# A two-layer hybrid trunk on one core: decay rows of the last x and z block from another queue, gates before weights, one combined pair less

## The chip, the core and the metric

The kernel runs on one core of one Trainium2 chip. A core has four engines that compute, each with its own list of instructions that it runs in order: TensorE (PE in the profile; its weight loads are PEld), VectorE (DVE), ScalarE (ACT) and GpSimd (POOL). SyncE (SP) only starts loads and stores. Loads can also be started from ScalarE's and GpSimd's lists. The metric is the device time of one execution in microseconds; lower is better. The median of the runs is compared.

## What is computed

The reference is a decoder trunk of two layers over 256 tokens of width 2048, in float32. Only its first layer's mixer is touched. Cut to that:

```python
proj = (xn @ w_in).astype(f32)
q, k, v, o, ig, fg, z, xbc, dt = jnp.split(proj, offs, axis=-1)
# eight mLSTM heads
hm = mlstm_chunkwise(q, k, v, i_pre, f_pre)
hm = rms_norm(hm, mlstm_norm) * jax.nn.sigmoid(o)
# 32 SSD heads
xbc = jax.nn.silu(causal_depthwise_conv(xbc, ssd_conv_w, ssd_conv_b))
y = ssd_chunked(xs, dt, a, bm, cm) + ssd_d[:, None] * xs
y = rms_norm(y * jax.nn.silu(z), ssd_norm)
mixed = jnp.concatenate([hm, y], axis=-1)
return mixed @ w_out
```

Behind it come the residual sum, a SwiGLU network of width 5632, a second layer with block attention (one block here, so plain causal attention), and a second SwiGLU network.

## The kernel before

**Products.** Every matrix product keeps float32 accuracy by splitting each operand into a high and a low part (`split`, L143 to L149: a cast on ScalarE and a subtraction on DVE) and adding three products (L303 to L305). Weights are fetched in pairs of two row groups of 128 by two column strips of 512. `weights` (L251) issues the loads and then the casts (L270) and subtractions (L275) of a pair. `block` runs over the eight pairs of a product and follows a plan, a string with one letter a pair. P is the direct form: 24 products of 512 columns. S is a combined form with seven block products in place of eight (21 products). For an S pair, sums of weights are also needed: SP loads one quarter, POOL loads another onto it with an accumulating load (L260, L261), and DVE makes two more additions (L285, L287). Sums of the activations are needed too (`activation_sums`, L235: four subtractions of 128 columns on DVE, a cast on ScalarE and a subtraction on DVE).

**Banks.** Four banks of PSUM take the direct products of a block, four others the extra products of the S pairs. Small work in between (turns of 128x128 blocks, scores, outputs of heads) uses these latter four when no S pair is at work.

**Order.** The program is written in order, and small jobs are queued with `later(wait, ...)`: they are written out after so many more pairs. While S pairs are at work, these jobs are held. A planner then orders each engine's list when the kernel is built. It takes the work that it believes ready, the earliest in the program first; `tc.high_priority(offset=n)` counts an instruction as written n earlier. The splitting of weights has an offset of 800, the emptying of banks 1600. Tiles come from a fixed number of slots by tag (three for sk, which holds q, k, activation sums and some decay rows; ten for s); who wants a slot waits until its last user is done.

**The first layer's mixer** runs in this order: B and C columns (two blocks), x and z columns (four blocks, `xz_block`), q and k of the first four heads, the output projection of the SSD part, then v, o (gate), q and k, v, o for the mLSTM heads, and the output projection of the mLSTM part (`project(w_out, 0, mx, PLAN["w2"], done1)`: two blocks of 1024 output columns).

**Decay rows.** `decay_rows` (L651) fetches, for two heads, their row of cumulated decays from a scratch tensor in HBM and spreads it over all 128 partitions, in two loads of 256 KB and 128 KB. DVE then adds the causal mask (L659), ScalarE takes the exponential (L664, L665), DVE multiplies by the step sizes and the scores of B and C (L710). For each block s of x and z, `ssd_decay` (L702) is written out four times, from the third pair of the next block on, so eight loads a block. All are issued from POOL's queue. The same block also has `x_pair`, in which TensorE turns the columns of x (L466), ScalarE and DVE convolve (L470, L476, L480, L481), and TensorE turns them back (`p_xs`, L699).

**Gates.** `o_block` (L840) multiplies the o columns into the heads. `gathered` completes the four tiles of 128 tokens by 512 columns, ScalarE takes the tanh (L850), DVE makes (tanh + 1) times the head (L851). `turn_strip` queues for each strip of 512 columns two jobs of `transpose_split` (L215): eight turns on TensorE, then copies with gain (L229), casts and subtractions. They give the pairs 0 to 7 of `mx`, two a strip; the first `o_block` makes 0 to 3, the second 4 to 7. A pair named in `mx.sums` (L774) gets its activation sums at once; another one's are made by `summed` when its S pair is first met (which first adds high and low part again, L205). `project` (L869) asks for the sums of all S pairs of the second block as soon as the first block's products are in.

Of the kernel before, what the change touches and what calls it, by code (L numbers as in the profile page):

```python
# [12 lines left out]
OP = mybir.AluOpType  # L13
# [4 lines left out]
P = 128  # L18
T = 256
NT = T // P  # L20
# [8 lines left out]
MH, MDK, MDV = 8, 128, 256  # L29
# [6 lines left out]
SPACE = {"raw": 6, "sum": 2, "wh": 6, "wl": 6, "xa": 8, "sk": 3, "s": 10, "vh": 2, "ph": 1}  # L36
PLAN = {
    "bc": "PPPPPPPP", "xz": "PPPPPPPP", "qk0": "PPPPPPPP", "w1": ("PSPSPSPP", "PSPSPSPP"),
    "v0": "PPPSPSSP", "o": "PPPSPSSP", "qk1": "PPPSPSSP", "v1": "PPPSPSSP", "w2": ("PPPSPSSP", "PPPSPSSP"),
    "x": "PSPSPSSP", "x0": "PPPSPSSP", "down4": ("PSPSPSSP", "PSPSPSSP"), "down3": ("PSPSPP", "PSPSPP"),  # L40
    "av0": "PPPSPSSP", "aq": "PPPSPSSP", "av1": "PPPSPSSP", "wo": ("PPPPPPPP", "PPPSPSSP"),
}
# [19 lines left out]
def hybrid_trunk(ctx: ExitStack, tc: tile.TileContext, a: dict, out: bass.AP):  # L62
    nc = tc.nc
# [16 lines left out]
    def home(tag):  # L80
        return lambda shape, name, dt=F32: big.tile(shape, dt, tag=tag, name=name, bufs=SPACE[tag])

    xa_home, sk_home, s_home, vh_home = home("xa"), home("sk"), home("s"), home("vh")
    ph_home = home("ph")

    def t2(shape, name, dt=F32):
        return tmp.tile(shape, dt, tag="tmp", name=name, bufs=9)
# [42 lines left out]
    G_MIX0, G_FFN0, G_MIX1, G_FFN1, G_ML, G_SS, G_CB = 0, 16, 32, 48, 64, 80, 96  # L130
# [32 lines left out]
    def later(wait, name, fn, *args):  # L163
        pending.append((clock[0] + wait, len(pending), name, fn, args))
# [13 lines left out]
    def need(name):  # L178
        if any(q[2] == name for q in pending):
            assert not held[0], name  # L180
            run_until(lambda p: not any(q[2] == name for q in pending))
# [64 lines left out]
    def turn_strip(kt, s, src, gcol, wait, step=0):  # L246
        for i in range(2):
            later(wait + i * step, (kt.name, 2 * s + i), transpose_split, kt, 2 * s + i,
                  [x[:, i * T:(i + 1) * T] for x in src], gcol)
# [130 lines left out]
    def gathered(F, pre):  # L380
        for i in (0, 2, 1, 3):
            if pre is None:
                yield i // 2, i % 2, F[i]
            else:
                with tc.high_priority(offset=1600):
                    (nc.vector.tensor_sub if i == 2 else nc.vector.tensor_add)(pre[i], F[i], pre[i])
                yield i // 2, i % 2, pre[i]
# [34 lines left out]
    def first_pair(src, turns_after, warm):  # L422
        raw = []
        for w, col in src:
            raw.append(home("raw")([P, 2, STRIP], "raw"))
            nc.sync.dma_start(raw[-1], w[:2 * P, col:col + STRIP].rearrange("(a p) f -> p a f", p=P))
        b = xt0.pair(0)
        pt = aux_bank("p_tr")
        with tc.issue_after(turns_after):
            for i in range(2):  # L430
                for t in range(NT):
                    turned = nc.tensor.transpose(pt[:, i * T + t * P:i * T + (t + 1) * P],
                                                 xin[t][:, i * P:(i + 1) * P], ident).ins
        with tc.issue_after(turned):
            warm_up(warm)
        pair = pt.rearrange("p (a b) -> p a b", a=2)
        high = [home("wh")([P, 2, STRIP], "wh", F32R) for _ in raw]
        low = [home("wl")([P, 2, STRIP], "wl", F32R) for _ in raw]

        def staged(s, k):  # L440
            with tied(last[0], cast[0]):
                split(high[s][:, k, :], low[s][:, k, :], raw[s][:, k, :])
            cast[0], last[0] = fresh

        for k in range(2):
            g = pv[:, G_MIX0 + k:G_MIX0 + k + 1]
            with tied(last[0], cast[0]) if k else ExitStack():
                split(b[:, k, 0, :], b[:, k, 1, :], pair[:, k, :], g)
            cast[0], last[0] = fresh
            staged(0, k)  # L450
        for k in range(2):
            staged(1, k)
        return [[(h[:, k, :], l[:, k, :]) for k in range(2)] for h, l in zip(high, low)]
# [57 lines left out]
    with tc.high_priority(offset=2000):  # L511
        first = first_pair(((w_in, C_B), (w_in, C_C)), rows_turned, WARM[1])
# [72 lines left out]
    scr = drp.tile([SH + MH, T], F32, name="scr")  # L585
# [62 lines left out]
    later(2, "gates", gate_chain)  # L648
    later(8, "gates", gate_columns)

    def decay_rows(first, home):  # L651
        need("gates")
        rb = home([P, 2, W3], "rows2")
        for lo, l0, n in ((0, 0, T), (T, P, P)):
            nc.gpsimd.dma_start(rb[:, :, lo:lo + n],
                                bass.AP(tensor=scr.tensor, offset=scr.offset + first * T + l0,
                                        ap=[[0, P], [T, 2], [1, n]]))
        for lo in (0, T):
            nc.vector.tensor_add(rb[:, :, lo:lo + P], rb[:, :, lo:lo + P],  # L659
                                 mask_sl[:, None, :].to_broadcast([P, 2, P]))  # L660
        return rb

    def decay(e, bias):
        nc.scalar.activation(e[:, :T], e[:, :T], AF.Exp, bias=bias[0])  # L664
        nc.scalar.activation(e[:, T:], e[:, T:], AF.Exp, bias=bias[1])  # L665
        return e
# [7 lines left out]
    def xz_block(s):  # L674
        got = block(((w_in, C_X + s * STRIP), (w_in, C_Z + s * STRIP)), xt0, 0, PLAN["xz"])
        tok = [None] * NT
        zg = sk_home([P, NT, STRIP], "zg")
        for t, i, src in gathered(*got):
            if i == 0:
                tok[t] = scaled(t, src, r0_)  # L680
            else:
                th = t2([P, STRIP], "thz")
                with tc.high_priority(offset=1600):
                    nc.scalar.activation(th, src, AF.Tanh, scale=rh0[:, t:t + 1])
                    nc.scalar.activation(zg[:, t, :], src, AF.Copy, scale=rh0[:, t:t + 1])
                nc.vector.scalar_tensor_tensor(zg[:, t, :], th, 1.0, zg[:, t, :], op0=OP.add, op1=OP.mult)
        y = vh_home([P, NT, STRIP], "y")
        for j in range(2):
            later(1 + j, ("x", s), x_pair, s, j, [x[:, j * T:(j + 1) * T] for x in tok], y)
        for j in range(4):  # L690
            later(2 + j, ("y", s), ssd_decay, s, j, y, zg)
# [10 lines left out]
    def ssd_decay(s, j, y, zg):  # L702
        need("cb")
        h0 = 8 * s + 2 * j
        es = decay_rows(MH + h0, s_home if j % 2 else sk_home)
        for hh in range(2):
            h = h0 + hh
            e = decay(es[:, hh, :], [ncols[:, t, CCS + h:CCS + h + 1] for t in range(NT)])
            for t, sl in ((0, slice(0, T)), (1, slice(T, W3))):
                nc.vector.scalar_tensor_tensor(e[:, sl], e[:, sl], cols[:, t, CDT + h:CDT + h + 1],  # L710
                                               cb[h // 8][:, (h // 4) % 2, sl], op0=OP.mult, op1=OP.mult)
        later(1, ("y", s), ssd_out, s, j, es, y, zg)
# [58 lines left out]
        nc.scalar.copy(dst, pt.rearrange("p (a b) -> p a b", a=2))  # L771

    mx = KT("mx", KD, s_home, {j: sk_home for j in range(KD // 2)})
    mx.sums = {5: None, 6: None}  # L774
    vh, em = {}, {}

    def qk_block(g, plan):
# [62 lines left out]
    def o_block(g, plan):  # L840
        for i in range(2):
            later(1 + g + i, ("hm", g), mlstm_out, 2 * g + i)
            later(min(2 + g + i, 3), ("hm", g), mlstm_norm, 2 * g + i)
        got = block(((w_in, C_O + 2 * g * STRIP), (w_in, C_O + (2 * g + 1) * STRIP)), xt0, 0, plan)
        need(("hm", g))
        gate = {}
        for t, i, src in gathered(*got):
            th = t2([P, 2, MDV], "tho") if got[1] is None else src.rearrange("p (a b) -> p a b", a=2)
            with tc.high_priority(offset=1600 if got[1] is None else 400):
                nc.scalar.activation(th, src.rearrange("p (a b) -> p a b", a=2), AF.Tanh, scale=rh0[:, t:t + 1])  # L850
            nc.vector.scalar_tensor_tensor(th, th, 1.0, vh[2 * g + i][:, t, :, :MDV], op0=OP.add, op1=OP.mult)  # L851
            gate[i, t] = th.rearrange("p a b -> p (a b)")
        for i in range(2):
            turn_strip(mx, 2 * g + i, [gate[i, t] for t in range(NT)], G_ML, 2)

    xr_ = xin

# [41 lines left out]
    project(w_out, D, sx, PLAN["w1"])  # L899
    v_block(0, PLAN["v0"], 1)  # L900
    o_block(0, PLAN["o"])
    qk_block(1, PLAN["qk1"])
    v_block(1, PLAN["v1"], 3)
    o_block(1, PLAN["o"])
    xt1, ss1, done1 = next_x("1", G_FFN0, {1: vh_home, 3: vh_home, 5: sk_home, 6: ph_home})
    project(w_out, 0, mx, PLAN["w2"], done1)
# [255 lines left out]
```

## Time and profile before

| | |
|---|---|
| median of 3 runs | 2551.51 us |
| lowest and highest | 2548.26 and 2552.74 us |
| the profiled execution | 2548.43 us |
| its span, first to last instruction | 2546.7 us |
| mean granted clock of TensorE | 0.998 |
| moved by DMA | 631.51 MB, mean 248 GB/s |
| loads of decay rows from POOL's queue | 20 of 256 KB and 20 of 128 KB |

Times in the rows are microseconds from the first instruction. A row of the order of time has the start, the duration, the engine, the line, the operation, what it writes and reads, and how many such instructions follow one another; in square brackets stand the idle time of the engine before it and what ended it. An engine's name with a q is its queue: it issues a load and does no computing. A row of waits has the engine and line that waited, what it waited for, the sum, the count and the longest. A row of a window has the window, its length, the busy time and count of PE, PEld, DVE, ACT and POOL, the granted clock, the share of the 16 DMA engines, and GB/s.

### The profile page before, as it was taken

To read this page: it belongs to the slowest core of one execution; us is meant where nothing else is said; L and a number is where in the kernel's file an instruction comes from. 1 tells how busy PE (TensorE), PEld (TensorE's weight loads), DVE (VectorE), ACT (ScalarE), POOL (GpSimd) and SP (SyncE) were. 2 spreads that over 40 slices of the span, in tenths; PEclk is the share of its full clock that TensorE was granted. 3 is DMA by queue.
4 is the path that set the end of the run, shared out by engine and by line. 5 is a ranking of instruction groups with operands and counts; after the bars stand their busy time and mean duration, and the time that the engine had idled before them with its cause. 6 is when DMAs were issued, how large, how long until landed. Compare 5 with 4: busy or idle time off the path is not lost.

```text
span 2546.7 us, 34498 instructions
## 1 busy us (share of the span) xinstructions
PE 2525.5 (99%) x11553; PEld 2083.3 (82%) x11553; DVE 2237.2 (88%) x2978; ACT 1601.3 (63%) x2160; POOL 366.8 (14%) x452
## 2 busy tenths in 40 slices
PE   9999999999999999999999999999999999999998
PEld 8888878888878888888888888888888888888887
DVE  6877778978799999999999888988899999999998
ACT  6566656566667665566656666656676656665664
POOL 2101211111111111111111111110011111111110
PEclk9999999999999999999999999999999999999999
DMA  8656668878778999999999887876689999999995
GB/s 281 185 167 189 195 182 257 259 224 254 224 222 252 277 273 283 278 272 276 273 290 270 262 249 230 243 229 208 191 243 282 265 289 275 277 266 296 291 267 175
DMA packets 333665, 631.51 MB, mean 248 GB/s; under 512 B 27256, under 2 KB 29824, under 8 KB 333488
## 3 DMA queue, kind: packets, MB, share of 16 engines
q1 hardware_dynamic: 278928, 527.71, 62.1%
q0 software_dynamic: 53376, 99.76, 22.3%
q8 instruction: 91, 1.49, 0.2%
q10 hardware_dynamic: 1184, 1.84, 0.2%
q14 instruction: 86, 0.70, 0.1%
HBM read 627.07 MB, written 2.14 MB: 247 GB/s over the span
## 4 chain that ended last, share of the span: by engine, by line
PE 95%; DVE 3%; DMA 1%; issue 1%; ACT 0%; POOL 0%; SPq 0%; POOLq 0%; DVEq 0%; ACTq 0%
PE acc_f L303 24%; PE acc_f L305 24%; PE acc_f L304 24%; PE acc_e L303 6%; PE acc_e L305 6%; PE acc_e L304 6%; PE p_tr L215 2%; DVE wl L275 1%; PE p_y L725 1%; PE p_qt L770 0%; PE p_num L814 0%; DMA raw<-in_l_ffn_down 0%; ACT wh L270 0%; DMA rows<-scr 0%; PE p_o L1038 0%
## 5 line engine op out<-in xcount | busy, mean ns | idle before, releaser
L270 ACT CAST wh<-raw 128x1024 fp32r<-128x1024 f32 (+1 forms) x1084 | 1049.5, 982 | 644.4 <-PE acc_f L305 283.8
L275 DVE TENSOR_TENSOR wl<-raw,wh 128x1024 fp32r<-128x1024 f32 (+1 forms) x1084 | 1211.3, 1135 | 189.2 <-ACT wh L270 177.4
L303 PE MATMUL acc_f<-wh,x 128*128 128x512 f32 x1168 | 457.0, 391 | 0.0
L305 PE MATMUL acc_f<-wh,x 128*128 128x512 f32 x1168 | 456.8, 391 | 0.0
L304 PE MATMUL acc_f<-wl,x 128*128 128x512 f32 x1168 | 456.8, 391 | 0.0
L270 ACT CAST wh<-sums 128x1024 fp32r<-128x1024 f32 x174 | 183.0, 1052 | 149.8 <-PE acc_f L305 87.4
L303 PE MATMUL acc_f<-wh,xa 128*128 128x512 f32 x678 | 270.1, 399 | 0.8 <-ACT wh L145 0.8
L305 PE MATMUL acc_f<-wh,xa 128*128 128x512 f32 x678 | 265.1, 391 | 0.0
L304 PE MATMUL acc_f<-wl,xa 128*128 128x512 f32 x678 | 264.8, 391 | 0.0
L305 PEld LDWEIGHTS acc_f<-wh,x 128*128 128x128 f32 x1168 | 219.4, 188 | 44.9
L304 PEld LDWEIGHTS acc_f<-wl,x 128*128 128x128 f32 x1168 | 219.5, 188 | 44.7
L303 PEld LDWEIGHTS acc_f<-wh,x 128*128 128x128 f32 x1168 | 219.4, 188 | 44.5
L275 DVE TENSOR_TENSOR wl<-sums,wh 128x1024 fp32r<-128x1024 f32 x174 | 212.1, 1219 | 27.3 <-ACT wh L270 26.9
L303 PE MATMUL acc_e<-wh,sk 128*128 128x512 f32 x522 | 206.3, 395 | 0.1
L304 PE MATMUL acc_e<-wl,sk 128*128 128x512 f32 x522 | 203.6, 390 | 0.0
L305 PE MATMUL acc_e<-wh,sk 128*128 128x512 f32 x522 | 202.7, 390 | 0.0
L261 POOL DMA_DIRECT2D sums<-in_l_ffn_gate x86 | 74.4, 865 | 765.7 <-DMA sums<-in_l_ffn_up 413.7
L305 PEld LDWEIGHTS acc_f<-wh,xa 128*128 128x128 f32 x678 | 127.5, 188 | 27.2
L304 PEld LDWEIGHTS acc_f<-wl,xa 128*128 128x128 f32 x678 | 127.8, 189 | 25.7 <-DVE wl L146 0.4
L303 PEld LDWEIGHTS acc_f<-wh,xa 128*128 128x128 f32 x678 | 127.6, 188 | 25.9 <-ACT wh L145 1.0
L285 DVE TENSOR_TENSOR raw<-raw,sums 128x512 f32<-128x512 f32 x174 | 118.9, 683 | 8.4 <-DMA sums<-in_l_ffn_down 5.8
L303 PEld LDWEIGHTS acc_e<-wh,sk 128*128 128x128 f32 x522 | 98.0, 188 | 29.4 <-ACT xg L226 6.8
(336 smaller groups left out, 4075.6 us busy)
## 6 DMA issues: line engine op xcount, KB each, us to landing
raw<-in_l_w_in SPq DMA_DIRECT2D x177, 512.0 KB, 4.7
raw<-in_l_ffn_gate SPq DMA_DIRECT2D x176, 512.0 KB, 6.2
raw<-in_l_ffn_down SPq DMA_DIRECT2D x136, 512.0 KB, 7.1
raw<-in_l_ffn_up SPq DMA_DIRECT2D x90, 512.0 KB, 6.5
sums<-in_l_ffn_up SPq DMA_DIRECT2D x172, 256.0 KB, 4.5
raw<-in_l_w_qkv SPq DMA_DIRECT2D x78, 512.0 KB, 6.4
raw<-in_l_w_out SPq DMA_DIRECT2D x52, 512.0 KB, 5.9
sums<-in_l_ffn_gate POOLq DMA_DIRECT2D x86, 256.0 KB, 6.8
```

The lines of the kernel that those rows point to most:

```text
L215: turned = nc.tensor.transpose(pt[:, i * T + t * P:i * T + (t + 1) * P], src[t][:, i * P:(i + 1) * P], ident)
L261: nc.gpsimd.dma_start(sums[:, i, :], other, accum_op=OP.add)
L270: cast[0] = nc.scalar.copy(h[:, :n, :], of[:, :n, :]).ins
L275: last[0] = nc.vector.tensor_sub(l[:, :n, :], of[:, :n, :], h[:, :n, :].bitcast(F32)).ins
L285: nc.vector.tensor_add(b[:, 1, :], b[:, 0, :], sums[:, 0, :])
L303: nc.tensor.matmul(dst, ah, bh, start=start, stop=False, **kw)
L304: nc.tensor.matmul(dst, ah, bl, start=False, stop=False, **kw)
L305: nth[0] = nc.tensor.matmul(dst, al, bh, start=False, stop=stop, **kw).ins
L725: nc.tensor.matmul(py[:, o0:o0 + SHD], e[:, lo:lo + P], y[:, st, hs], start=st == 0, stop=st == t, skip_group_check=True)
```

## The change

The two loads of `decay_rows` take the queue as a parameter: POOL's as before, but ScalarE's for the last x and z block (s == 3). In `o_block` the tanh and the product get one priority, 1200, where the tanh had 400 (1600 in a plan without S, which isn't used for it) and the product none; both now stand ahead of the splitting of weights. For the first gate block the second strip is turned one pair later than the first. In the first block of the mLSTM part's output projection pair 6 is direct, so that two pairs are combined, 3 and 5; the second block keeps three. The pairs whose activation sums are made at once are 3 and 5, not 5 and 6.

```diff
-    "v0": "PPPSPSSP", "o": "PPPSPSSP", "qk1": "PPPSPSSP", "v1": "PPPSPSSP", "w2": ("PPPSPSSP", "PPPSPSSP"),
+    "v0": "PPPSPSSP", "o": "PPPSPSSP", "qk1": "PPPSPSSP", "v1": "PPPSPSSP", "w2": ("PPPSPSPP", "PPPSPSSP"),
...
-    def decay_rows(first, home):
+    def decay_rows(first, home, queue=nc.gpsimd):
...
-            nc.gpsimd.dma_start(rb[:, :, lo:lo + n],
+            queue.dma_start(rb[:, :, lo:lo + n],
...
-        es = decay_rows(MH + h0, s_home if j % 2 else sk_home)
+        es = decay_rows(MH + h0, s_home if j % 2 else sk_home, nc.scalar if s == 3 else nc.gpsimd)
...
-    mx.sums = {5: None, 6: None}
+    mx.sums = {3: None, 5: None}
...
-            with tc.high_priority(offset=1600 if got[1] is None else 400):
+            with tc.high_priority(offset=1200):
                 nc.scalar.activation(th, src.rearrange("p (a b) -> p a b", a=2), AF.Tanh, scale=rh0[:, t:t + 1])
-            nc.vector.scalar_tensor_tensor(th, th, 1.0, vh[2 * g + i][:, t, :, :MDV], op0=OP.add, op1=OP.mult)
+                nc.vector.scalar_tensor_tensor(th, th, 1.0, vh[2 * g + i][:, t, :, :MDV], op0=OP.add, op1=OP.mult)
...
-            turn_strip(mx, 2 * g + i, [gate[i, t] for t in range(NT)], G_ML, 2)
+            turn_strip(mx, 2 * g + i, [gate[i, t] for t in range(NT)], G_ML, 2 + i * (1 - g))
```

More of the change, by code (lines that the diff above doesn't have):

```diff
@@ L654, in decay_rows @@
         for lo, l0, n in ((0, 0, T), (T, P, P)):
-            nc.gpsimd.dma_start(rb[:, :, lo:lo + n],
-                                bass.AP(tensor=scr.tensor, offset=scr.offset + first * T + l0,
-                                        ap=[[0, P], [T, 2], [1, n]]))
+            queue.dma_start(rb[:, :, lo:lo + n],
+                            bass.AP(tensor=scr.tensor, offset=scr.offset + first * T + l0,
+                                    ap=[[0, P], [T, 2], [1, n]]))
         for lo in (0, T):
```

## The prediction

> **What bounds the kernel now.** I read the page first, then the list of waits on TensorE (PE), then the order of time on each engine at the places that list names.
>
> ```profile
> span 2546.7 us, 34498 instructions
> PE 95%; DVE 3%; DMA 1%; issue 1%; ACT 0%; POOL 0%; SPq 0%; POOLq 0%; DVEq 0%; ACTq 0%
> ...
> PE p_xs L699 <- DVE xs L481: 5.6, 1, 5.6
> PE p_tr L215 <- DVE pre L851: 2.7, 7, 0.8
> PE acc_f L303 <- ACT wh L270: 1.9, 2, 1.1
> ```
>
> The chain that ends last is 95% TensorE: the kernel is a row of matrix products, and a change pays only where TensorE stands, or in the number of its products. It stands at few places, and the three longest entries of the waits are one for each part of this change: the turning of the convolved x (p_xs), the turning of the gated heads (p_tr from pre), and the first output block (acc_f waiting for a cast). Busy time hides some of the loss, since the ends of products are modelled, so I measure every stop from the starts.
>
> ```profile
> 307.59 0.39 PE L303 MATMUL acc_f<-wh,xa 128*128 128x512 f32 x1
> ...
> 312.12 0.39 PE L305 MATMUL acc_f<-wh,xa 128*128 128x512 f32 x1
> ...
> 277.23 0.60 PE L699 MATMUL p_xs<-ident,xs 128*128 128x128 f32 x4
> ...
> 327.20 0.39 PE L305 MATMUL acc_f<-wh,xa 128*128 128x512 f32 x1
> 333.23 1.09 PE L699 MATMUL p_xs<-ident,xs 128*128 128x128 f32 x4 [5.63 <-DVE xs L481]
> ...
> 336.16 0.40 PE L305 MATMUL acc_f<-wh,xa 128*128 128x512 f32 x1
> ...
> 334.00:336.00 2.00, 2.00 (x7) 1.61 (x6) 2.00 (x5) 0.63 (x2) 0.00 (x0) 0.50 1.04 214
> ```
>
> The first two rows are the first and last of 21 products in a row: 20 steps in 4.53 us, so one product of 512 columns costs 0.2265 us. The third row is the turn p_xs one x/z block earlier, with no wait before it. In the last block TensorE is free for it at 327.20 + 0.23 = 327.43 and starts at 333.23: **5.80 us** lost. Then the granted clock is 0.50 (last row): from 333.23 to 336.16 four turns and five products take 2.93 us, where four turns at 0.109 (below) and five products make 1.57: another **1.36 us**. Together 7.16 us.
>
> **Part 1: the decay rows.** Why is DVE late there, and only there?
>
> ```profile
> 255.82 5.77 POOL L655 DMA_DIRECT2D rows<-scr  x8
> ...
> 306.96 0.70 POOL L141 TENSOR_TENSOR rrg<-rs,mhalf 128x2 f32<-128x2 f32 x1 [13.40 <-DVE rs L140]
> 312.25 1.83 POOL L261 DMA_DIRECT2D sums<-in_l_w_out  x2 [4.58 <-DMA sums<-in_l_w_out]
> 313.98 4.42 POOL L655 DMA_DIRECT2D rows<-scr  x6
> 319.48 0.71 POOL L655 DMA_DIRECT2D rows<-scr  x1 [1.08 <-DMA sums<-in_l_w_out]
> ...
> 322.20 0.43 DVE L659 TENSOR_TENSOR rows<-rows,phase 128x256 f32<-128x256 f32 x1 [5.65 <-DMA rows<-scr]
> ...
> 332.40 0.68 DVE L481 SCALAR_TENSOR_TENSOR xs<-thc,cv 128x512 f32<-128x512 f32 x1
> ```
>
> In the block before, all eight row loads leave POOL's queue in one stretch at 255.82. One block is 51.8 us long (the p_xs above comes at 277.23, so its like is due at about 329), and the same point here is 307.6, just as POOL ends its power at 307.66. But here POOL's next entry is the accumulating load of the first combined pair of the following projection, which waits for SP's plain load to land; the rows leave 6.3 us late, at 313.98, the last two later still. DVE has the mask addition of the rows (L659) at the head of its list and stands 5.65 us, and all that follows on DVE, up to xs at 332.40 + 0.68, runs without a break. So each microsecond that the first rows land earlier is one microsecond less on TensorE, until 5.80 are gone.
>
> The change takes these eight issues off POOL (5.77 us of its time, which nobody waits for) and puts eight on ScalarE. What they cost there, and when they land:
>
> ```profile
> DMA to landing us min/median/max: 4.6/6.8/9.4
> ...
> 2328.11 1.04 ACT L270 CAST wh<-raw 128x1024 fp32r<-128x1024 f32 x1
> 2328.69 0.33 ACTq L1061 DMA_DIRECT2D gf<-in_final_norm  x1
> 2329.05 0.61 ACT L270 CAST wh<-raw 128x512 fp32r<-128x512 f32 x1
> ...
> 255.00:268.00 13.00, 13.00 (x63) 10.75 (x62) 8.97 (x17) 11.57 (x20) 6.42 (x9) 1.00 0.87 258
> ...
> 313.00:327.00 14.00, 14.00 (x67) 11.50 (x66) 7.47 (x13) 7.96 (x14) 6.82 (x10) 1.00 0.89 263
> ```
>
> The first row is of the rows' own loads. A load issued from ScalarE's queue (2328.69) runs under the cast before it, and the next cast follows without a gap: 8 x 0.33 = 2.6 us of issue, nothing of it on the path as long as casts or copies lie beside it, 2.6 us of ScalarE if that cover is gone. The unknown is where in ScalarE's list the planner puts them. At best they go where POOL was free, 307.7, and land at 312.3 to 317.1: the stop vanishes. At worst they go behind the copies that empty the banks at the end of the block, 314 or later, and land no earlier than now: nothing gained. DVE needs them at 322.20 - 5.80 = 316.4. Nothing in the trace says which, so I take the middle, 310.8, and the median landing, 6.8: 317.6, so 1.2 us stays, too short a stop for the slow clock, of which I see nothing behind stops of about 1 us. Gain 7.2 - 1.2 = **6.0**, ends 0 and 7.2, and a loss in the last rival below. The waiting instructions behind such a load on ScalarE would be these same bank copies and the casts, and TensorE waits for both.
>
> On the landing, the Trainium skill speaks against the change: "DMA: Bandwidth & Descriptors", section "Issuing engines are not separate DMA queues", says that loads from ScalarE, SP and GpSimd run on the same 16 DMA engines and interleave, and that another issuer saves only the time of issuing. The share of 0.89 in the last row above fits it. By that rule alone the gain would be the issue delay, 6.3 us at most, and nothing if the bytes are the limit: the first rival.
>
> **Part 2: gates ahead of weights.**
>
> ```profile
> 558.62 0.29 PE L215 MATMUL p_tr<-ident,pre 128*128 128x128 f32 x1
> ...
> 562.14 0.48 PE L303 MATMUL acc_f<-wh,xa 128*128 128x512 f32 x1
> ...
> 696.20 0.39 PE L305 MATMUL acc_f<-wh,mx 128*128 128x512 f32 x1
> ...
> 700.45 0.48 PE L303 MATMUL acc_f<-wh,mx 128*128 128x512 f32 x1
> ...
> 739.78 0.87 PE p_tr L215 x8
> ...
> 551.44 1.94 ACT L850 ACTIVATE pre<-pre,rh 128x512 f32<-128x512 f32 x3
> 557.84 1.29 DVE L851 SCALAR_TENSOR_TENSOR pre<-pre,v 128x512 f32<-128x512 f32 x2
> ```
>
> Eight turns cost 0.87 us undisturbed (0.109 each), sixteen 1.74. After the first gate block they take 562.14 - 558.62 = 3.52: **1.78** lost; after the second, 700.45 - (696.20 + 0.23) = 4.02: **2.28** lost. The tanh is done at 553.4, but the DVE product (L851) comes at 557.84, behind the splitting of weights. With one priority above the weights' 800, both come first and the turns find their input some 3 us ahead. The weights move back by four tanh (1.94 / 3 = 0.65 each) and four products (0.65 each), 2.6 us on each engine; the pair being split there is used one pair later, at least 5 us away (24 x 0.2265), so I cost this at nothing; uncovered, it is 2.6 us per block.
>
> In the first half the second strip is turned one pair later, immediately before the first combined pair: same eight turns, but its copies out of two banks now meet products that want these banks. Undisturbed that is nothing; the bound above is one strip's copies, four of about the size of a tanh, 2.6 us. I take 0.5, near the lower end, since a combined pair begins with three products into a bank that the turns don't use. Gain 1.78 + 2.28 - 0.5 = **3.6**, ends -1.1 and 4.1.
>
> **Part 3: one combined pair less, sums made early.**
>
> ```profile
> 713.26 0.39 PE L305 MATMUL acc_e<-wh,mx 128*128 128x512 f32 x1
> ...
> 714.40 0.50 PE L303 MATMUL acc_f<-wh,mx 128*128 128x512 f32 x1 [0.75 <-ACT wh L270]
> ...
> 716.99 0.50 PE L303 MATMUL acc_f<-wh,mx 128*128 128x512 f32 x1 [1.13 <-ACT wh L270]
> ...
> 703.51 0.68 DVE L205 TENSOR_TENSOR xg<-mx 128x512 f32<-128x512 f32 x1
> ...
> 713.65 0.28 DVE L238 TENSOR_TENSOR sf<-xg 128x128 f32<-128x128 f32 x1
> ...
> 716.85 0.62 ACT L145 CAST sk<-sf 128x512 fp32r<-128x512 f32 x1
> ...
> L275 DVE TENSOR_TENSOR wl<-sums,wh 128x1024 fp32r<-128x1024 f32 x174 | 212.1, 1219 | 27.3 <-ACT wh L270 26.9
> L285 DVE TENSOR_TENSOR raw<-raw,sums 128x512 f32<-128x512 f32 x174 | 118.9, 683 | 8.4 <-DMA sums<-in_l_ffn_down 5.8
> ```
>
> From 713.26 to 716.99 four products are issued in 3.73 us instead of 0.91: **2.8** lost. DVE has three sets of activation sums to make inside this block; that of pair 3 starts at 703.51 and its cast comes at 716.85. Pair 6 taken directly needs 24 products for 21: +3 x 0.2265 = **0.7** on TensorE. DVE drops from 3 x 1.22 + 3 x 0.68 to 2 x 1.22 for that pair (three whole and one half subtraction, the addition at L285 and its like at L287), 3.3 us less. Pair 3's sums go three blocks earlier, pair 6's to the start of the second output block, each 4 x 0.28 + 0.68 = 1.8 us of DVE and 0.62 of ScalarE, where the waits of TensorE name nothing but the turns. Pair 3's tile then holds one of the three sk slots until the projection; q and k need the other two, so I cost that at nothing, and if a third were wanted its writer would wait, which the sum leaves out and the range takes in. SP issues two loads in place of four, POOL none in place of two. I expect the stop gone but for 0.2: 2.8 - 0.7 - 0.2 = **1.9**, ends -0.7 and 2.1.
>
> **The sum.** 6.0 + 3.6 + 1.9 = 11.5; I take 11, as every list is planned anew. The profiled execution took 2548.43 us (span 2546.7 and 1.7 around it), so 2537.4 by its own measure; it lies 3.1 below the median 2551.51 of the runs shown, so for a median I forecast 2540.5, in its own range 2535 to 2545.
>
> **The rivals.**
> *The bytes are the limit, or the rows come late in ScalarE's list* (first rival). For it: DMA share 0.89 in the window, and two accumulations beside the rows. Against it: in the block before, the rows left at 255.82 into a share of 0.87 (the window's row beside the other) and were in time; only the issue was earlier. Rows gain 0, the rest 5.5: 2546.0.
> *Gates and sums gain nothing*: what DVE does first makes the weights late, and the stops move to the products. For it: both engines run in order; against it: the 5 us of lead. Rows 6.0 - 0.7 = 5.3: 2546.2.
> *The change does not do what it says*: new planning returns the stops elsewhere: 2551.5.
> *Slower: ScalarE held by its own loads.* A load at the head of ScalarE's list that waits (as the row at 319.48 waited on POOL for an unrelated landing) stops the bank copies behind it. Place: end of the last x/z block. Two such waits in series at the longest landing, 9.4, hold ScalarE 18.8 us, where now the hold is 5.65; a hold there passes to TensorE one for one, so +13.1 - 5.5 = +7.6: 2559. It decides from a hold of 5.65 + 5.5 = 11.2 us on. Against it: an earlier landing frees it sooner, and 4.6 is as likely as 9.4.
>
> **How the numbers follow.** A change within 0.2%, 5.1 us, can't be told from none. Forecast 0.58, all faster. First rival 0.16, half faster and half same (2546.0 against the bound 2546.4). Second (2546.2) 0.11: 0.06 faster, 0.05 same. No effect 0.08, same. Slower 0.07: 0.05 slower, 0.02 same. That is faster 0.72, same 0.23, slower 0.05. The range leaves out no effect and slower, and the ends of the forecast: 2534 (all three parts in full, 7.2 + 4.1 + 2.1 = 13.4, and runs low) to 2548.5.
>
> **What would show it.** Part 1: rows issued under ACTq in the last block, DVE's idle before L659 near 322 under 2 us, no 0.50 clock there. Part 2: L851 within 3 us of its tanh, sixteen turns in under 2.2 us. Part 3: 24 products for pair 6, no stop over 0.5 us in the first output block. Wrong: L659 still waiting for rows, or new waits of PE on copies out of banks just before combined pairs.

## The result and the profile after

The changed kernel takes 2538.64 us (median; 2538.14 to 2539.95), the kernel before 2552.12 on the same chip (2548.26 to 2555.27): ratio 0.9949, 95% interval 0.9931 to 0.9966. The forecast was 2540.5 in a range of 2534.0 to 2548.5, faster, which it is, by 0.5%. The profiled execution took 2539.95, the highest of the four, and its span is 8.9 us less than the one before. The profiled execution of the kernel before (2548.43) was one of its shorter ones, so the comparison of the two traces shows less than the medians do. First the page of the changed kernel, its span and the shares of the chain:

```profile
span 2537.8 us, 34480 instructions
...
PE 94%; DMA 2%; DVE 2%; issue 1%; ACT 1%; POOL 0%; POOLq 0%; DVEq 0%; ACTq 0%
```

Then the three longest entries in the list of TensorE's waits (what it waited for: us in total, times, longest):

```profile
PE p_xs L699 <- DVE xs L481: 1.8, 1, 1.8
PE warm L122 <- POOL phase L105: 1.0, 1, 1.0
PE acc_f L303 <- DVE pre L386: 0.7, 1, 0.7
```

Of the three entries on which the prediction rested, p_xs is down from 5.6 to 1.8, and the waits of the gates' turns (2.7) and of the first output block (1.9) are gone. A new one stands there: acc_f, a product that waits for an addition on DVE that empties a bank.

**The rows**, from the order of time on ScalarE's queue, on DVE and on TensorE, and from the windows (us, TensorE busy and instructions, the same for the other engines, granted clock, DMA share, GB/s):

```profile
310.95 0.41 ACTq L655 DMA_DIRECT2D rows<-scr  x1
...
315.52 0.38 ACTq L655 DMA_DIRECT2D rows<-scr  x1
...
328.18 0.43 ACTq L655 DMA_DIRECT2D rows<-scr  x1
```

```profile
315.71 0.42 DVE L659 TENSOR_TENSOR rows<-rows,phase 128x256 f32<-128x256 f32 x1 [1.27 <-DMA rows<-scr]
...
321.15 0.43 DVE L659 TENSOR_TENSOR rows<-rows,phase 128x256 f32<-128x256 f32 x1 [1.57 <-DMA rows<-scr]
```

```profile
328.54 0.39 PE L303 MATMUL acc_f<-wh,xa 128*128 128x512 f32 x1
330.74 0.63 PE L699 MATMUL p_xs<-ident,xs 128*128 128x128 f32 x4 [1.81 <-DVE xs L481]
```

```profile
330.00:334.00 4.00, 3.26 (x23) 3.04 (x24) 4.00 (x9) 3.79 (x9) 0.07 (x1) 1.00 1.06 280
```

The eight loads are spread over 17 us (310.95 to 328.18), one by one between ScalarE's casts and copies, some of which wait for TensorE and DVE; GpSimd had issued six of them in one stretch. The first lands 4.7 us after its issue and the DVE mask addition (L659) begins at 315.71, where it began at 322.20. The second load, the other half of the same two heads, leaves ScalarE's list only at 315.52 and lands at 321.13, so DVE stands 1.57 us more for it. At p_xs 330.74 - 328.54 - 0.23 = 1.97 us are left of 5.80, and the clock stays at 1.00.

**The gates**, on ScalarE, on DVE, and on TensorE at the turns:

```profile
543.62 0.72 ACT L850 ACTIVATE pre<-pre,rh 128x512 f32<-128x512 f32 x1 [0.42 <-DVE pre L386]
```

```profile
546.43 1.29 DVE L851 SCALAR_TENSOR_TENSOR pre<-pre,v 128x512 f32<-128x512 f32 x2
```

```profile
553.31 1.04 PE L215 MATMUL p_tr<-ident,pre 128*128 128x128 f32 x8
554.10 0.48 PE L303 MATMUL acc_f<-wh,xa 128*128 128x512 f32 x1
```

The products (L851) now follow the tanh within 3 us (546.43 behind 543.62; it was 557.84 behind 551.44), and the eight turns take 554.10 - 553.31 = 0.79 us without a stop. In the second gate block the price shows, on DVE and on TensorE:

```profile
679.48 0.69 DVE L851 SCALAR_TENSOR_TENSOR pre<-pre,v 128x512 f32<-128x512 f32 x1 [2.59 <-ACT pre L850]
680.09 1.88 DVE L386 TENSOR_TENSOR pre<-acc_f,pre 128x512 f32<-128x512 f32 x3
```

```profile
679.73 0.39 PE L305 MATMUL acc_f<-wh,mx 128*128 128x512 f32 x1
680.83 0.50 PE L303 MATMUL acc_f<-wh,mx 128*128 128x512 f32 x1 [0.71 <-DVE pre L386]
```

The product that waits for its tanh stands ahead of three additions that empty banks, DVE is idle 2.59 us with them behind it, and TensorE, which wants a bank, loses 680.83 - 679.73 - 0.23 = 0.87 us.

**The pair**: the window of the first output block shows TensorE busy through all of it (697 to 718, 93 products and turns, clock 1.00):

```profile
697.00:718.00 21.00, 21.00 (x93) 1.00 0.92 259
```

Matching the starts of the same turns in both traces gives where the time went; the difference is called the offset below. Past the last x and z block the changed kernel is 5.25 us further ahead than it was before that block. It loses 0.2 on the way to the turns of the gates and gains 1.6 there; at the end of the first output block it is 3.5 more ahead: 10.1 in all at 780. Of that it loses 2.4 again between 1400 and 1660, in stages whose lists are the same in both kernels.

### The profile page after: what moved, and what is told of

It is laid out like the page before. It is cut to its first block, busy times and chain, and to the rows that moved or that the text cites. A ratio compares the mean times of both kernels' runs of the same rounds, so it can differ in the third digit from the quotient of the medians.

```text
span 2537.8 us, 34480 instructions
## 1 busy us (share of the span) xinstructions
PE 2525.1 (99%) x11556; PEld 2083.2 (82%) x11556; DVE 2236.1 (88%) x2974; ACT 1600.5 (63%) x2158; POOL 359.1 (14%) x442
## 4 chain that ended last, share of the span: by engine, by line
PE 94%; DMA 2%; DVE 2%; issue 1%; ACT 1%; POOL 0%; POOLq 0%; DVEq 0%; ACTq 0%
PE acc_f L303 24%; PE acc_f L305 24%; PE acc_f L304 24%; PE acc_e L303 6%; PE acc_e L305 6%; PE acc_e L304 6%; PE p_tr L215 2%; PE p_y L725 1%; DMA raw<-in_l_w_qkv 1%; DVE wl L275 1%; DMA rows<-scr 1%; ACT wh L270 0%; PE p_qt L770 0%; DMA raw<-in_l_ffn_down 0%; DMA raw<-in_l_w_out 0%
```

## The experiments

Medians in us, and the ratio to the kernel before on the same chip with its 95% interval ("rows", "gates" and "plan" are the three parts of the change):

```
rows alone              2547.16  0.9982 (0.9973 to 0.9992)
gates alone             2551.34  0.9997 (0.9988 to 1.0006)
plan alone              2548.13  0.9990 (0.9980 to 0.9999)
rows + gates            2545.61  0.9979 (0.9970 to 0.9988)
rows + plan             2540.34  0.9963 (0.9951 to 0.9974)
gates + plan            2544.02  0.9974 (0.9964 to 0.9983)
all three, again        2539.09  0.9956 (0.9943 to 0.9970)
rows first on GpSimd    2542.43  0.9958 (0.9946 to 0.9971)
that + gates + plan     2536.47  0.9948 (0.9935 to 0.9960)
that, gates tied        2537.07  0.9949 (0.9937 to 0.9961)
all, sums of 3 late     2541.83  0.9964 (0.9952 to 0.9977)
```

The kernel before had medians of 2550.6, 2550.92 and 2550.0 beside them.

### Each part alone

**The rows alone**:

```diff
...
-        es = decay_rows(MH + h0, s_home if j % 2 else sk_home)
+        es = decay_rows(MH + h0, s_home if j % 2 else sk_home, nc.scalar if s == 3 else nc.gpsimd)
```

> The kernel before with only the eight row loads of the last x and z block on ScalarE's queue; gates and plan as before. Theory (the issue was late, nothing else): TensorE's stop at p_xs goes from 5.8 to about 2.0 us as in the changed kernel, the half clock behind it goes, and the offset against the kernel before is about -5.3 us right after that place (5.25 was read between the two traces) and stays so to the end: 0.9979 of the time before. Rival (the parts lean on each other: the p_xs stop only gets short because the first output block is planned otherwise): the stop stays above 4 us and the time is within 2 us of before. Rival (ScalarE held by its loads): new stops of TensorE on copies or casts at the end of the last block, more than 3 us in sum, and no gain.

Past the last x and z block this kernel was 6.95 us ahead of the one before, 6.6 of it won there (stop at p_xs 0.63 us): the theory's gain and more. But in the profiled execution the lead did not stay: 5.1 at the first turn of the gates, 2.4 at 635, none at 783. The order of time on TensorE shows where:

```profile
551.44 0.39 PE L305 MATMUL acc_f<-wh,xa 128*128 128x512 f32 x1
553.55 0.33 PE L215 MATMUL p_tr<-ident,pre 128*128 128x128 f32 x1 [1.72 <-DVE pre L851]
554.15 0.98 PE L215 MATMUL p_tr<-ident,pre 128*128 128x128 f32 x7 [0.28 <-DVE pre L851]
555.89 2.14 PE L215 MATMUL p_tr<-ident,pre 128*128 128x128 f32 x8 [0.76 <-DVE pre L851]
```

and on ScalarE and in the windows (TensorE alone) what was late, and what followed:

```profile
545.45 1.05 ACT L270 CAST wh<-raw 128x1024 fp32r<-128x1024 f32 x1 [2.86 <-DMA raw<-in_l_w_in]
546.41 1.95 ACT L850 ACTIVATE pre<-pre,rh 128x512 f32<-128x512 f32 x3
```

```profile
558.00:562.00 4.00, 4.00 (x11) 0.50 1.03 215
```

TensorE comes to the turns 7 us earlier, but the tanh stands in ScalarE's list behind a cast that waits 2.86 us for weights to land, and they land 5 us earlier, not 7. So the stops at the turns grow from 1.78 us to 3.6, and the clock goes to 0.50 during the last of them: a product takes 0.427 us from start to start in place of 0.2265, until 562. In all 6.4 us are lost between 550 and 600, where the kernel before loses 1.8. The 11 executions spread from 2542.71 to 2551.88, and go with their mean granted clock: 2542.7 to 2546.6 at 0.999 (4), 2550.3 to 2551.9 at 0.997 and 0.996 (3). The profile is of the one of 2550.34, among the three slowest. That the half clock comes behind these stops in some executions and not in others fits these clocks, but no trace of a faster execution shows it.

**The gates alone**:

```diff
-            with tc.high_priority(offset=1600 if got[1] is None else 400):
+            with tc.high_priority(offset=1200):
...
-            nc.vector.scalar_tensor_tensor(th, th, 1.0, vh[2 * g + i][:, t, :, :MDV], op0=OP.add, op1=OP.mult)
+                nc.vector.scalar_tensor_tensor(th, th, 1.0, vh[2 * g + i][:, t, :, :MDV], op0=OP.add, op1=OP.mult)
...
-            turn_strip(mx, 2 * g + i, [gate[i, t] for t in range(NT)], G_ML, 2)
+            turn_strip(mx, 2 * g + i, [gate[i, t] for t in range(NT)], G_ML, 2 + i * (1 - g))
```

> The kernel before with only the gates' priority and the later turn of the second strip; rows on GpSimd and plan as before. Theory: the p_xs stop stays at 5.8 us; the sixteen turns after each gate block take under 2.2 us, where they took 3.52 and 4.02, so the two gate places give back 1.8 and 2.3 us; against that the DVE product that waits for its tanh stands ahead of the additions that empty the banks, and TensorE stops some 0.9 us there near 680. Net -2.5 to -3.5 us: 0.9988. Rival (my prediction's price): -3.6 us, with no new stop. Rival (the delay only moves): weights come later by 2.6 us a block, the offset at the end of the first output block is 0, same time.

No change, as the second rival said, and worse in the trace: the turns run through, 1.6 us are gained at the first block, and the 0.86 us stop near 686 is there; then the first output block takes all and more. TensorE there, and DVE's list:

```profile
711.37 0.40 PE L305 MATMUL acc_e<-wh,mx 128*128 128x512 f32 x1
712.80 0.50 PE L303 MATMUL acc_f<-wh,mx 128*128 128x512 f32 x1 [1.03 <-ACT wh L270]
715.01 0.50 PE L304 MATMUL acc_f<-wl,mx 128*128 128x512 f32 x1 [1.72 <-DVE wl L275]
...
716.88 0.80 PE L303 MATMUL acc_f<-wh,mx 128*128 128x512 f32 x1 [1.13 <-ACT wh L270]
```

```profile
704.17 0.69 DVE L205 TENSOR_TENSOR xg<-mx 128x512 f32<-128x512 f32 x1
...
715.47 0.29 DVE L241 TENSOR_TENSOR sf<-xg,sf 128x128 f32<-128x128 f32 x1
716.86 1.23 DVE L275 TENSOR_TENSOR wl<-raw,wh 128x1024 fp32r<-128x1024 f32 x1 [1.10 <-ACT wh L270]
```

From 704.17 to 715.47 DVE has no idle time: work on three sets of sums and six splits stand in one row. The cast on ScalarE for the next split starts at 715.78, just as the last subtraction of that row ends (715.47 + 0.29), and the split that TensorE waits for comes at 716.86, where it came at 716.97 in the kernel before. TensorE has come earlier to the same queue. Its stops there grow from 2.7 to 4.9 us (1.20, 1.99, 1.30, 0.37), and now a half clock follows (12 steps, 2.4 us). Between 700 and 750 the kernel loses 8.3 us, before 3.0.

**The plan alone**:

```diff
-    ... "w2": ("PPPSPSSP", "PPPSPSSP"),
+    ... "w2": ("PPPSPSPP", "PPPSPSSP"),
...
-    mx.sums = {5: None, 6: None}
+    mx.sums = {3: None, 5: None}
```

> The kernel before with only the first output block's plan (pair 6 with three products) and the sums made for pairs 3 and 5. Theory: the 2.8 us lost near 714 to 717 go, three more products cost 0.7, so the offset past 740 is about -2 us: 0.9992. Rival: the sums of pair 3, made three blocks earlier, or the casts of pair 6, cost as much somewhere else before 740; offset 0 and no change. Rival (the gain of 3.5 us in the second gate stretch of the changed kernel is the plan's and not the gates'): offset -3 or more, and gates_only shows nothing there.

The loss in the block falls from some 3 us to under 0.5, the three added products cost 0.7, and the offset moves by 2.3 us over the block: the theory. The median is 2.5 us lower, its interval nearly touches 1. The gain is all in the removed stops; at p_xs this execution lost 1.0 us more than the kernel before, nearly all of it to a longer half clock.

### Two at a time

The edits are those above, two of three.

> The changed kernel without the plan's part (rows on ScalarE and gates early; pair 6 still combined, sums for 5 and 6). The three single runs add up to -3.4 + 0.7 - 2.5 = -5.2 us by their medians, and the changed kernel stands at -12.0, so 6.8 us belong to no part alone. Theory (the stops lean on each other: without the early gates the rows' gain is lost again at the turns of the gates, without the plan the gates' gain is lost again in the first output block, where DVE runs without a break from 703 to 719): the rows' 7 us now last past both gate blocks, no stop above 1 us at the turns; in the first output block stops of 4 to 6 us in a row return and a half clock behind them. Offset -8 us at 640, -4 to -6 at the end; median 2545 to 2547. Rival (sizes add): -3.4 + 0.7, 2547.9, and the turns of the gates stop as in the kernel before. Rival (the plan's part adds only its 2.5): 2541.1.

> The changed kernel without the rows' part. Theory: the p_xs stop stays at 4.2 to 5.8 us; the turns of the gates run through; the 8.3 us that the gates alone lost in the first output block go, because DVE no longer has three sets of sums in it; only the 0.87 us near 686 stays. Offset -4 to -5 us at the end, median 2545.5 to 2547. Rival (sizes add): +0.7 - 2.5 = -1.8, 2548.8, with stops of TensorE on splits left in the first output block.

> The changed kernel without the gates' part. Theory: TensorE comes 7 us earlier to the turns of the gates, but the tanh stands behind a cast that waits for weights to land, so it stops there 3 us and more at both gate blocks with a half clock behind it, as with the rows alone (6.4 and 4.3 us lost in these stretches); the first output block is clean. Offset -7 at 540, -2 to -4 at 690, -5 to -6 at the end; median 2544.5 to 2546. Rival (sizes add): -5.9, 2544.7, but with stops at the turns no longer than the 1.8 and 2.3 us of the kernel before; here the trace decides, not the time. Rival (the gates are worth nothing beside the other two): 2539.

Rows and gates: as expected. 9.0 us ahead behind the second gate block's turns, then the same four stops as with the gates alone (1.20, 1.99, 1.30, 0.36) and the half clock behind them; 3.9 are left at 779. Gates and plan: the block's loss is 0.3 us, and 2544.02 is better than was expected. So the plan is worth 0.10% alone, and 0.23% beside the gates (0.9974 against 0.9997).

Rows and plan missed: 2540.34, better than any theory but the last rival's. The stops at the turns were there (1.5 and 2.5 us in sum), but shorter than with the rows alone, and no half clock followed, so nothing was given back. The cast ahead of the tanh got its weights at 544.19, 1.3 us earlier than with the rows alone; which of the two is the rule for these lists was not tried. Beside the other two parts the gates are worth 0.07 to 0.14%, within the intervals.

### Whose fault the rows were

**All eight rows first on GpSimd's queue**: the kernel before, with the accumulating loads put behind the last row load in the same list.

```diff
-                    nc.gpsimd.dma_start(sums[:, i, :], other, accum_op=OP.add)
+                    with tied(*[r for r in row_load if r is not None]):
+                        nc.gpsimd.dma_start(sums[:, i, :], other, accum_op=OP.add)
...
-            nc.gpsimd.dma_start(rb[:, :, lo:lo + n],
+            row_load[0] = nc.gpsimd.dma_start(rb[:, :, lo:lo + n],
...
```

> The kernel before, rows still on GpSimd's queue, but the accumulating loads of the next projection's combined pairs tied behind the last row load, so that all eight rows stand ahead of them in GpSimd's list. Theory (it was the order in GpSimd's list, not the queue): rows leave by 308 and the first land by 313 to 316, the p_xs stop and the half clock go entirely, offset -6 to -7 us past that place, 1 to 2 us better than rows_only, unless the combined pair that now gets its sum later makes TensorE stop near 330 to 345 by the same amount. Rival (the bytes are the limit: the 16 DMA engines are busy 0.89 there): rows leave earlier but land no earlier than 319, and the stop stays above 3 us. Rival (it must be another queue because the issue itself holds GpSimd): rows leave in one stretch of 5.8 us but the accumulations then come too late and TensorE loses 3 us or more to a combined pair; no gain.

GpSimd's list, and DVE's (L657 and L661 are the row loads and their mask addition; this kernel has two lines more):

```profile
308.05 0.74 POOL L657 DMA_DIRECT2D rows<-scr  x1
308.95 5.03 POOL L657 DMA_DIRECT2D rows<-scr  x7 [0.15 <-issue]
314.41 0.93 POOL L263 DMA_DIRECT2D sums<-in_l_w_out  x1 [0.43 <-DMA rows<-scr]
```

```profile
315.05 0.42 DVE L661 TENSOR_TENSOR rows<-rows,phase 128x256 f32<-128x256 f32 x1
...
316.92 0.41 DVE L661 TENSOR_TENSOR rows<-rows,phase 128x256 f32<-128x256 f32 x1
```

The rows leave at 308.05, 5.9 us earlier, the mask addition begins 7.15 us earlier, and DVE never stands for them. The stop at p_xs is gone entirely and the offset past it is 7.2 us. With one edit of order this kernel is at 0.9958: 2542.43 us, 4.7 under the rows alone on ScalarE's queue, where 1 to 2 had been expected. At the turns of the first gate block it stops 2.4 us in sum with no half clock behind, where the profiled execution of the rows alone stops 3.6 with one. The accumulating loads come 2 us later, and no combined pair waits for them. So the bytes were not the limit, and another queue was not needed. This agrees with the Trainium skill, DMA: Bandwidth & Descriptors, section Issuing engines are not separate DMA queues: another issuer saves the time of issuing only. What was saved here was 5.9 us in the issuing engine's list, most of it an unrelated wait that stood ahead of the rows.

**The same with gates and plan**, without and with one tie more:

```diff
...
-        for t, i, src in gathered(*got):
+        for t, i, src in list(gathered(*got)):
...
-                nc.vector.scalar_tensor_tensor(th, th, 1.0, vh[2 * g + i][:, t, :, :MDV], op0=OP.add, op1=OP.mult)
+                with tied(gathered_last[0]):
+                    nc.vector.scalar_tensor_tensor(th, th, 1.0, vh[2 * g + i][:, t, :, :MDV], op0=OP.add, op1=OP.mult)
```

The tie puts the products behind the last of the additions that empty the banks.

> Plan and gates as in the changed kernel, the rows on GpSimd's queue with all eight ahead of the accumulating loads; without the tie of the gates. Theory (the order in GpSimd's list was the fault, ScalarE's queue a detour): the p_xs stop is gone, the 0.87 us near 680 is back, the two stops of 0.78 and 0.65 us at 686 and 698 that the tie brought are not there: 2536.5 to 2537.5, 1 to 2 us under the changed kernel, the same as with the tie. Rival (ScalarE's queue as good): 2538.6.

> Plan and gates as in the changed kernel; the rows on GpSimd's queue, all eight ahead of the accumulating loads; and the first product of a gate tied behind the last addition that empties a bank. Theory: no stop at p_xs (1.97 us less), none at the third addition out of a bank near 680 (0.87 less), the rest as in the changed kernel: 2538.6 - 2.8 = 2535.8. Rival (the tie makes the gates late again): stops at the turns of the gates, 2 us or more, no gain over the changed kernel. Rival (combined pairs of the next projection wait for their sums): a new stop between 335 and 350.

Without the tie: 2536.47, the fastest of all, 2.6 us under the changed kernel beside it (their runs overlap: 2535.53 to 2539.93 and 2537.66 to 2540.01). There is no stop above 0.3 us between 8 and 1590 us. The 0.87 us near 680 that was expected there did not come: the tanh was in time. The tie brought stops of its own, 0.78 us at 685.93 and 0.65 at 698.51, and gains nothing.

### What in the plan's part does it

```diff
-    mx.sums = {3: None, 5: None}
+    mx.sums = {5: None}
```

> The changed kernel, but with the sums of pair 3 made inside the first output block as before (only pair 5's early); pair 6 as three products. It tells the two halves of the plan's part apart: pair 6's sums, splits and additions on DVE are gone, pair 3's are still there. Theory (what held TensorE is the sum of DVE's work between the turns and the third combined pair; pair 6's share of it, with its sums 1.8 and its splits 3.3 us, is the larger): the four stops of 4.9 us in the first output block shrink to under 1.5, no half clock, time within 1.5 us of the changed kernel: 2538.6 to 2540. Rival (the sums of pair 3 are what blocks, as the first combined pair waits for them): stops of 2 us or more before the products of pair 3, 2541 to 2546.

The rival was right:

```profile
702.66 0.40 PE L305 MATMUL acc_f<-wh,mx 128*128 128x512 f32 x1
704.91 0.50 PE L303 MATMUL acc_f<-wh,sk 128*128 128x512 f32 x1 [1.85 <-ACT sk L145]
```

The second row is the first product that takes the sums of pair 3 (sk); it waits 2.02 us for them, and 1.6 us of half clock follow. Without pair 6 as a combined pair the other stops are gone, but the sums of pair 3 have to be early as well. The time is 2.7 us above that of the changed kernel beside it. Both halves of the part are needed.

### What a stop costs

**The changed kernel again**, and with idle work on DVE ahead of twelve splittings:

> The changed kernel once more, with a second profile. Theory: the 2.4 us that its first profile lost against the kernel before between 1400 and 1660, where both kernels have the same lists, belong to that execution and not to the change; a second profile has them elsewhere or not at all, while the stop at p_xs (1.8) and the one at the third addition out of a bank (0.7) return. Median 2538 to 2540. Rival (something of the change reaches those stages): the same offsets are lost at the same places again.

```diff
             if not summed:
+                for _ in range(stops.pop(min(stops, default=999)) if min(stops, default=999) <= calls[0] else 0):
+                    with tied(last[0]):
+                        last[0] = nc.vector.tensor_add(idle, idle, idle).ins
```

> The changed kernel with twelve stretches of idle work on DVE (8 to 24 additions of 448 columns that nothing reads) ahead of a splitting of weights in the two feed-forward stages, so that TensorE stops there for different lengths. It measures when the half clock follows a stop. So far stops of 5.8 us, of 4.4, and of 3.3 in three pieces were followed by 2 to 5 us at 0.50; stops of 2.0 in one piece, and of 2.1 to 2.8 in three, by none. Theory: a limit near 3 us, above which every stop costs 2 to 3 us more, whatever its length. By the Trainium skill, TensorE: Matmul & The Clock Gate, section What's actually happening, the clock halves after at least one idle window of 3.4 us, and the windows run freely: by that rule stops between 3.4 and 6.8 us would be followed by the half clock in some cases and not in others, and stops below 3.4 us never. Rival (the loss grows with the length of the stop): no limit, time at 0.50 in proportion.

The second profile of the changed kernel has 0.93 us at p_xs and none near 680; it is 12.1 us ahead at 771 and loses 1.7 later, at 946 and at 1600. So the places of the late loss differ, except one: products that wait for the softmax (p_o) near 1600 stop 0.7 to 1.7 us in nine of the fourteen profiles, both of the changed kernel among them, that of the kernel before not. The lists of that stage are the same in both kernels; why the stop comes and goes is open.

The kernel with idle work, by rows of TensorE that ended a stop, and by windows behind them (TensorE alone):

```profile
890.26 0.50 PE L312 MATMUL acc_e<-wh,x 128*128 128x512 f32 x1 [1.50 <-ACT wh L275]
891.21 0.49 PE L312 MATMUL acc_e<-wh,sk 128*128 128x512 f32 x1 [0.45 <-ACT wh L275]
...
995.00 0.50 PE L313 MATMUL acc_f<-wl,ha 128*128 128x512 f32 x1 [2.96 <-DVE wl L280]
...
1449.08 0.79 PE L313 MATMUL acc_f<-wl,ha 128*128 128x512 f32 x1 [9.02 <-DVE wl L280]
```

```profile
891.50:894.50 3.00, 3.00 (x14) 1.00 0.93 234
995.00:998.50 3.50, 3.50 (x10) 0.66 0.62 197
...
1449.50:1453.50 4.00, 4.00 (x10) 0.50 0.76 222
```

Measured from the starts, the twelve places have stops of 2.4 to 13.4 us in sum. Behind the one of 2.4 (1.66 + 0.72) the clock stays; behind the eleven of 3.1 and more 7 to 12 products take 0.427 us each, 3.0 to 5.1 us at 0.50, which costs 1.4 to 2.4 us: 1.4 behind 3.1, 1.8 behind 9.5 and 13.4. So the loss is not in proportion to the stop, and a little smaller than the 2 to 3 us of the theory. The theory's limit near 3 us doesn't hold as it stands: 3.0 us in four pieces left the full clock (the plan alone, at 697), and 2.4 in two, 6.9 us apart, brought the half clock (the sums of pair 3 late, at 705).

The granted clock itself tells why. In each of the fourteen traces it changes only at the edges of one even grid of 3.41 us, which lies differently in each execution, and it stays at 0.50 for one to four of these stretches. Two cases on their grids (edges rounded), the sums of pair 3 late and then the plan alone (TensorE alone):

```profile
702.81:706.22 3.41, 1.55 (x8) 0.99 0.89 214
706.22:709.63 3.41, 3.41 (x10) 0.51 0.91 277
709.63:713.05 3.42, 3.42 (x17) 1.00 0.80 240
...
696.60:700.00 3.40, 1.99 (x12) 1.00 0.00 0
700.00:703.40 3.40, 2.49 (x15) 1.00 0.52 172
```

From the starts, TensorE stands 2.13 us in the first of these stretches, and the next has the half clock. At 697 the 3.0 us fall into two stretches, 1.89 and 0.90 us, and nothing follows. At the first turns of the gates 2.48 us fall into one stretch with the rows alone, and 1.2 at most with rows and plan, which kept the full clock. Between the first 8 and the last 10 us, the fourteen traces have twenty stretches at full clock with stops of 2.1 us and more (2.11 the least), each followed by one at 0.50; of all the others, up to 2.07 us, none is. An estimate from that: a stop between 2.1 and 4.2 us calls the half clock or not by where it falls on the grid, a longer one always.

The rule of the Trainium skill, TensorE: Matmul & The Clock Gate, section What's actually happening, an idle window of about 3.4 us that runs freely, agrees with the trace in the length and the free running of the window. It does not agree in what the window must hold: by that rule a stop of 3.1 us would never call the half clock, and here it did, as did 2.13 us within one stretch, so the window needn't be idle throughout.

## Why the prediction was right, and where not

**The bound and the three places**: right. The stops were where the list of waits had them, and what came new was small (0.87 us at one bank) or in stages that the change leaves as they were.

**Part 1, 6.0 us**: 5.25 in the first profile, 6.1 in the second. The first row was issued at 310.95, where the middle of two bounds was 310.8. It landed sooner than the median taken (4.7 for 6.8), but the second load came late, and 1.97 and 0.93 us stayed where 1.2 was expected. That the first row's place was the middle of the two bounds is luck: the trace of before could not tell it, and the planner spread the eight loads over ScalarE's list. The first rival's two halves part here: the bytes were no limit, and rows late in ScalarE's list is what left the rest.

**Part 2, 3.6 us, and part 3, 1.9**: 1.6 at the first gate block (1.3 by the prediction's steps), and 3.5 and 4.5 us in the two profiles for the second block and the pair together, where the steps give 4.2. Of the 1.78 us at the first gate block all but 0.2 came back, where 0.5 had been set aside for the second strip's copies; the 0.87 us near 680, in one profile of two, was a wait that the prediction did not have: it priced the four products that move ahead on DVE by their length, and did not look at what is queued behind the one that waits for its tanh.

**The sum**: 11.5 forecast; 10.1 and 12.1 at 780 by the two profiles, of which 2.4 and 1.7 are lost later, in lists that the change leaves as they were. The medians are 13.5 and 10.9 below those of before beside them. For the profiled execution 2537.4 was forecast; the two took 2539.95 and 2537.66.

That the sum came out is in part luck, for its shares did not. Left out of the three one at a time, the rows cost 0.18 to 0.25%, the gates 0.07 to 0.14%, the plan 0.23 to 0.30%: 4.6 to 6.4, 1.8 to 3.6 and 5.9 to 7.7 us, where the sum has 6.0, 3.6 and 1.9. The plan, its smallest term, is worth most beside the others, since without it 5.1 us of what rows and gates win are lost again in the first output block; the gates' share lies within the intervals.

**What failed is that the terms were added as if each were its own.** "the pair being split there is used one pair later, at least 5 us away (24 x 0.2265), so I cost this at nothing" holds only with the plan's part beside it. Without it, the gates alone bring 2551.34, no change, as the rival "Gates and sums gain nothing" has it: the stops move to the products. The weights themselves did not come later (716.86 for 716.97); DVE's list from 704 to 715 has no gap, and TensorE comes earlier to the same wait. The rows alone lose most of their 7 us at the turns of the gates in the execution that has a trace, and 3.4 us are left by the median. The forecast was right because all three were made together; as a forecast of a single part its terms for the rows and the gates would have been wrong by 2.6 and 4.3 us (6.0 against 2550.6 - 2547.16, and 3.6 against 2550.6 - 2551.34). And 1.36 us for the slow clock at p_xs was one draw: behind the same stop it cost about 1 us more in two other executions (with the gates alone and the plan alone), since it holds for whole stretches of 3.41 us. It is called by 2.1 us of stops in one such stretch, so the prediction was right to expect none behind a stop of about 1 us.

## What to carry over

A stop that goes at one place makes the bounding engine come earlier to the next queue: ask at each place behind it whether the engine that feeds it moves along, or is itself full or waits for transfers, before the terms are added. Where a transfer is late, look first at what stands ahead of it in its own queue; putting the order right there gave here more than another queue (2542.43 against 2547.16 us alone; 2536.47 against 2539.09 beside the other parts, where the runs overlap), and without the spreading. Several short stops close together can cost more than their sum, when 2.1 us of them fall into one stretch of 3.41 us and call the slow clock.

## What was not expected of the hardware

The granted clock keeps to a grid of 3.41 us, and 2.1 us of stops within one stretch of it are enough for 0.50 in the next. Behind the stops made on purpose the clock at 0.50 lasts 3.0 to 5.1 us past their end, whatever their length (3.1 to 13.4 us). The time of one kernel goes with it: the rows alone take 2542.7 to 2551.9 us as the mean granted clock goes from 0.999 to 0.996. A load issued on ScalarE's queue takes 0.37 to 0.49 us of its queue, and in the changed kernel every gap of ScalarE beside the eight has a wait for TensorE or DVE as its end, none the issue.
